# A norm factor spread over 128 partitions by a store and a load in place of a product with ones

## The chip, the cores and the metric

The kernel runs on one core of one Trainium2 chip. The metric is the device time of one execution in microseconds; lower is better. Three executions of the kernel before took 2622.88, 2625.9 and 2628.31 us; the median, 2625.9, stands for it.

## The reference

One layer over 4096 latent tokens of width 1024, with 256 context tokens ahead of it. Every token is normed by its root mean square, scaled and shifted, and goes through one wide projection, from which two branches take their parts: a gated MLP that mixes positions in chunks of 128, and a gated linear attention in both directions. The branches are merged by gates and go through an output projection. What matters here is the first line:

```python
def rmsnorm(x, g):
    xf = x.astype(jnp.float32)
    y = xf * lax.rsqrt(jnp.mean(xf * xf, axis=-1, keepdims=True) + EPS)
    return (y * g.astype(jnp.float32)).astype(x.dtype)
...
        h = rmsnorm(x, norm_g[layer]) * (1 + scale[:, None]) + shift[:, None]
        p = h @ wi
        hc = rmsnorm(xc, norm_g[layer]) * (1 + mod_c[D_MODEL:2 * D_MODEL]) + mod_c[:D_MODEL]
        pc = hc @ (wi[:, K0:ZB0] if last else wi)
```

Everything is in float32.

## The kernel before

The tokens are worked in 32 tiles of 128. **Stage 1** (to about 780 us) makes the normed input of each tile and from it the parts of the projection that the attention and the chunk mixing need; it also runs both. **Stage 2** makes the other parts of the projection and the output from halves that stage 1 writes to DRAM (opd). The change is in stage 1 alone.

In stage 1 each tile's input is on the chip twice: x (tokens on partitions, one buffer) and hf (channels on partitions, 8 blocks of 128 channels by 128 tokens, three buffers). The norm factor of a token is made from x, where a token's channels lie in one partition: a Square on ACT with a sum (L136) gives ms, one number per partition, and two POOL instructions (L88, L89) turn it into the reciprocal root. The products need it on hf, where tokens lie along the free axis, so all 128 factors have to be in every partition. `scales` puts them on a diagonal (dg, DVE, L139), and `spread` multiplies ones by that diagonal on PE (L144), which gives rb in PSUM: each partition holds all 128 factors. `modulate` then multiplies hf by rb on DVE (L149, all 8 blocks at once) and scales and shifts block by block on ACT (L151, 8 instructions). ms and dg have two buffers each, so a tile's Square (which writes ms) can't run before the diagonal of two tiles earlier has been made, and that one not before the rb of two tiles earlier has been multiplied.

`parts` (L165) copies hf into a rounded part hh (ACT, L167) and a rest hl (DVE, L168) for the products, and forms sums of halves that go to opd. PE's products l, v and a of a tile (L378 to L380, three instructions per block of channels) read hh and hl; k and q (L388 to L390) are made for two tiles at once. So the loop goes over **pairs of tiles**. For each pair: l of the even tile gives the low-rank gate inputs (stk, plr, lrT), those of both tiles give pg (PE, L424), then e (Exp and Ln on ACT), a scan, decays (em, kd, qdp, kdec), the masked scores (psc on PE, at on DVE), the attention's output po (PE, L608) with its copy oi, and the state: pk (PE), its copy sk (ACT, L615), and S (DVE, L619), from which the next sk is made. pr (PE, L547) and sv are the chunk mixing. Names in the rows: mk, mq, ml, mv, ma are the products k, q, l, v, a in PSUM; x, hf, ms, dg, rb carry their tile's number.

Each engine runs its instructions in the order in which they were laid down when the kernel was built. That order is made by the framework's scheduler from the program, the dependencies and the number of buffers, not written by hand; only some attention steps are tied to the last product ahead of them (`behind`). SP issues loads and most stores, ACT issues the stores of pkd and svd; each of these queues is in order too, so an instruction that waits holds up what stands behind it.

The 256 context tokens (`scales_T`, `norm_c`) use `spread` as well, twice, at the very start. From the outer program, the lines that start and drive this:

```python
            looked = {0: look(0)}
...
            if i:
                prepare(i + 1)
            pr0 = project(i, 0, lrT, "lva")
...
            kept["k", u] = heads("k", f"_{u}", lambda: behind(i - 2))
            stage(i - 1)
            kept["q", u] = heads("q", f"_{u}", lambda: behind(i - 2))
            behind(i - 1)
            prepare(i + 2)
            pr1 = project(i + 1, 1, lrT, "lva")
```

Of the kernel before, what the change touches and what calls it, by code (L numbers as in the profile page):

```python
# [8 lines left out]
F32 = mybir.dt.float32  # L9
F32R = mybir.dt.float32r  # L10
U32 = mybir.dt.uint32
AF = mybir.ActivationFunctionType
ALU = mybir.AluOpType

P = 128
# [3 lines left out]
NT = SEQ // P  # L19
# [18 lines left out]
def block_kernel(ctx: ExitStack, tc, t, out):  # L38
    nc = tc.nc
    V, S, G, T, Q = nc.vector, nc.scalar, nc.gpsimd, nc.tensor, nc.sync  # L40

    cp = ctx.enter_context(tc.tile_pool(name="cp", bufs=1))
    dr = ctx.enter_context(tc.tile_pool(name="dr", bufs=1, space=bass.MemoryType.DRAM))
# [9 lines left out]
    gated = dr.tile([KT, P], F32, name="gated")  # L53
    csd = dr.tile([2 * KT, P], F32, name="csd")
    xhd = dr.tile([SEQ, 256], F32, name="xhd")

    banks = {}

    def psum(tag, shape, name):
        pool, n = banks[tag]  # L60
        return pool.tile(shape, F32, tag=tag, name=name, bufs=n)
# [7 lines left out]
    def const(name, shape, dt=F32):  # L69
        c = cp.tile(shape, dt, name="c_" + name)  # L70
        Q.dma_start(c, t[name])
        return c
# [13 lines left out]
    def rstd_of(dst, n):  # L86

        G.tensor_scalar(dst, dst, EPS, None, ALU.add)  # L88
        G.tensor_tensor(dst, dst, mhalf[:, :n], ALU.pow)  # L89
# [6 lines left out]
    with ExitStack() as c1:  # L96
# [7 lines left out]
        ph = c1.enter_context(tc.tile_pool(name="ph", bufs=2))  # L104
# [20 lines left out]
        def load_x(src, srcT, name):  # L125

            x = ph.tile([P, D], F32, tag="x", name="x" + name, bufs=1)
            Q.dma_start(x, src)
            hf = ph.tile([P, KT, P], F32, tag="hf", name="hf" + name, bufs=3)
            Q.dma_start(hf, srcT)  # L130
            return x, hf

        def scales(x, name):

            ms = ph.tile([P, 1], F32, tag="ms", name="ms" + name)
            S.activation(x, x, AF.Square, scale=1.0 / 32.0, accum_out=ms)  # L136
            rstd_of(ms, 1)
            dg = ph.tile([P, P], F32, tag="dg", name="dg" + name)
            V.tensor_scalar(dg, ident, ms, None, ALU.mult)  # L139
            return dg  # L140

        def spread(dg, name):
            rb = psum("t", [P, P], "rb" + name)
            T.matmul(rb, lhsT=ones, rhs=dg, start=True, stop=True)  # L144
            return rb

        def modulate(hf, rb, who):

            V.tensor_tensor(hf, hf, rb.unsqueeze(1).to_broadcast([P, KT, P]), ALU.mult)  # L149
            for k in range(KT):  # L150
                S.activation(hf[:, k, :], hf[:, k, :], AF.Identity, bias=AB[:, 0, k, who:who + 1],  # L151
                             scale=AB[:, 1, k, who:who + 1])

        def look(i):
            x, hf = load_x(t["x"][i * P:(i + 1) * P, :], t["xT"][i], f"_{i}")
            return hf, scales(x, f"_{i}")

        def ready(i):
            if i + 1 < NT:
                looked[i + 1] = look(i + 1)  # L160
            hf, dg = looked.pop(i)
            modulate(hf, spread(dg, f"_{i}"), 0)
            return hf

        def parts(i, hf):  # L165
# [17 lines left out]
        def prepare(i):  # L183
            parts(i, ready(i))


        with ExitStack() as c0:
# [91 lines left out]
            for g in range(4):  # L279
# [24 lines left out]
                if g == 0:  # L304
                    ident = const("ident", [P, P])
# [22 lines left out]
            load_w1("v", 256, 512)  # L328
            load_w1("l", 0, 272)
            looked = {0: look(0)}  # L330
            Q.dma_start(msk, t["msk"])
            Q.dma_start(dmask, t["dmask"])
# [136 lines left out]
        for c0 in (0, 256):  # L469
            for j in range(2):  # L470
                pvv = product(j, "v", c0, c0 + 256, f"mvc{j}{c0}")
                S.copy(vs[j][:, c0:c0 + 256], pvv)
        hf0 = ready(0)
        for j in range(2):
            pl = product(j, "l", 0, 272, f"mlc{j}")
# [188 lines left out]
        i = NT - 2  # L664
# [276 lines left out]
    for b in reversed(range(NSUP)):  # L941
# [16 lines left out]
        for c in range(KT):  # L958
# [5 lines left out]
            i = b * ST + ST - 1 - c  # L964
# [117 lines left out]
    for n, (b, half) in enumerate(steps):  # L1082
# [9 lines left out]
        for c in range(KT):  # L1092
# [15 lines left out]
            if half:  # L1108
                f = mo[:, c]
# [6 lines left out]
            f = pf.tile([P, BTOK], F32, tag="f", name=f"fm{nm}_{c}")  # L1116
# [224 lines left out]
```

## Time and profile before

| What | Before |
|---|---|
| Median of 3 executions | 2625.9 us (2622.88 to 2628.31) |
| The profiled execution | 2625.88 us |
| Its span in the profile | 2624.1 us |
| PE's granted clock, mean | 0.993 |
| POOL, all of its work in the span | 542.5 us in 514 instructions |
| HBM, mean over the span | 184 GB/s |

The span is what the profiler saw between the first and the last instruction; 1.78 us of the execution lie around it. PE is the matmul engine and PEld its weight loads, DVE, ACT and POOL the vector, scalar and general engines, SP the one that issues DMAs; ACTq and SPq in a row are those engines' instruction queues (a DMA issue stands there). A row of a timeline has start, length, engine, line, operation, output and inputs, shape and count, and in brackets how long the engine had been idle and what released it; a row of groups has count, busy time, mean length in ns, and idle time ahead of it. Lengths of matmuls overlap, as one starts before the last has drained; so on PE the distance between two starts is what one costs. A product of 128 x 128 by 128 x 272 starts about 0.127 us behind the last.

### The profile page before, as it was taken

How to read it: one execution, taken by the hardware profiler on the slowest of the kernel's cores; microseconds unless marked ns; L12 is line 12 of the kernel's file. 1: busy time of each engine (PE TensorE's matmuls, PEld its weight loads, DVE VectorE, ACT ScalarE, POOL GpSimd, SP SyncE). 2: the span in 40 equal slices, each digit the busy share in tenths (PEclk: the TensorE clock that was granted, in tenths of full speed). 3: DMA queues.
4: the chain of work that ended last, by engine and by line, in shares of the span. 5: the costliest groups of instructions: out<-in, count | busy, mean ns of one | idle time of the engine just before them, and what ended most of it. 6: DMA issues, size and time to landing. Idle time of an engine off the chain costs nothing.

```text
span 2624.1 us, 37671 instructions
## 1 busy us (share of the span) xinstructions
PE 2571.3 (98%) x13688; PEld 2202.0 (84%) x13688; DVE 1758.1 (67%) x2980; ACT 1213.1 (46%) x2478; POOL 542.5 (21%) x514
## 2 busy tenths in 40 slices
PE   8999999999988999999999999999999999999998
PEld 4899999999987778888888888888878888878887
DVE  6677777777787656775578557855678666565555
ACT  5666665656564444454445443544441011144443
POOL 2101010000002333233223333333310000032222
PEclk9999999999999999999999999999999999999999
DMA  8443434343349554554446444644359968676654
GB/s 287 152 137 128 144 125 153 125 152 120 119 128 253 197 181 155 194 208 154 135 160 229 153 150 150 229 149 164 121 192 338 340 223 271 232 258 222 224 201 145
DMA packets 248956, 485.37 MB, mean 185 GB/s; under 512 B 20551, under 2 KB 127327, under 8 KB 235074
## 3 DMA queue, kind: packets, MB, share of 16 engines
q1 hardware_dynamic: 189922, 416.88, 47.5%
q10 hardware_dynamic: 58848, 66.08, 7.6%
q8 instruction: 108, 1.77, 0.3%
q14 instruction: 78, 0.64, 0.1%
HBM read 303.56 MB, written 179.32 MB: 184 GB/s over the span
## 4 chain that ended last, share of the span: by engine, by line
PE 62%; DMA 4%; DVE 2%; issue 1%; ACT 1%; POOL 1%; SPq 0%; POOLq 0%; DVEq 0%; ACTq 0%
PE Xg L753 12%; PE Xa L753 6%; PE Wg L753 6%; PE poX L1188 6%; PE py L1037 4%; PE py L1035 4%; PE py L1036 4%; PE poW L1188 3%; PE Xz L753 3%; PE Wa L753 3%; PE Yg L753 3%; PE Wz L753 2%; PE Ya L753 1%; PE poY L1188 1%; DMA op<-opd 1%; PE po L849 1%
## 5 line engine op out<-in xcount | busy, mean ns | idle before, releaser
L1188 PE MATMUL poX<-wo,mop 128*128 128x512 f32 x768 | 176.2, 390 | 2.0 <-DVE mop L1179 2.0
L1188 PEld LDWEIGHTS poX<-wo,mop 128*128 128x128 f32 x768 | 144.0, 188 | 32.7 <-DVE mop L1179 2.8
L1194 POOL TENSOR_TENSOR so<-so,xo 128x512 f32<-128x512 f32 x48 | 71.3, 1500 | 418.4 <-ACT so L1193 366.6
L727 POOL TENSOR_TENSOR rg<-rg 128x512 f32<-128x512 f32 x32 | 46.3, 1447 | 399.3 <-DMA rg<-in_wq 352.0
L1106 DVE TENSOR_TENSOR sg<-sg,py 128x512 f32<-128x512 f32 x128 | 86.6, 683 | 62.0 <-PE py L1037 60.5
L1179 DVE TENSOR_TENSOR mop<-mr,mop 128x1024 fp32r<-128x1024 f32 x56 | 73.2, 1307 | 70.3 <-ACT mop L1178 69.9
L151 ACT ACTIVATE hf<-hf,AB 128x128 f32<-128x128 f32 x256 | 102.4, 481 | 29.3 <-DVE hf L149 29.3
L1025 ACT CAST ah<-al 128x512 fp32r<-128x512 f32 x32 | 17.6, 618 | 210.2 <-DMA al<-abd 144.8
L378 PE MATMUL mv<-w_vh,hh 128*128 128x512 f32 x256 | 101.7, 397 | 0.6 <-ACT va L524 0.6
L1037 PE MATMUL py<-bh,wbl 128*128 128x512 f32 x256 | 99.7, 390 | 0.9 <-DVE wbl L1016 0.9
L1035 PE MATMUL py<-bh,wbh 128*128 128x512 f32 x256 | 100.0, 390 | 0.7 <-ACT wbh L1015 0.6
L380 PE MATMUL mv<-w_vh,hl 128*128 128x512 f32 x256 | 100.1, 391 | 0.0
L379 PE MATMUL mv<-w_vl,hh 128*128 128x512 f32 x256 | 100.1, 391 | 0.0
L1036 PE MATMUL py<-bl,wbh 128*128 128x512 f32 x256 | 99.7, 389 | 0.0
L1035 PE MATMUL py<-ah,wbh 128*128 128x512 f32 x256 | 99.7, 389 | 0.0
L1037 PE MATMUL py<-ah,wbl 128*128 128x512 f32 x256 | 99.6, 389 | 0.0
L1036 PE MATMUL py<-al,wbh 128*128 128x512 f32 x256 | 99.6, 389 | 0.0
L753 PE MATMUL Xg<-op,w1g 128*128 128x512 f32 x384 | 97.9, 404 | 0.5 <-DVE w1g L749 0.5
L753 PE MATMUL Xg<-op,w6g 128*128 128x512 f32 x384 | 93.3, 391 | 5.1 <-ACT s1g L758 4.9
L753 PE MATMUL Wg<-op,w5g 128*128 128x512 f32 x384 | 94.0, 391 | 3.4 <-ACT w5g L748 2.1
L753 PE MATMUL Yg<-op,w2g 128*128 128x512 f32 x384 | 93.8, 390 | 0.0
L753 PE MATMUL Xg<-op,w7g 128*128 128x512 f32 x384 | 92.8, 390 | 0.0
(418 smaller groups left out, 7732.3 us busy)
## 6 DMA issues: line engine op xcount, KB each, us to landing
rg<-in_wq SPq DMA_DIRECT2D x32, 1024.0 KB, 5.5
gd<-fg SPq DMA_DIRECT2D x128, 256.0 KB, 2.4
sg<-gd SPq DMA_DIRECT2D x64, 512.0 KB, 4.8
op<-opd SPq DMA_DIRECT2D x28, 1024.0 KB, 5.9
mr<-md SPq DMA_DIRECT2D x56, 512.0 KB, 3.6
opd<-hf SPq DMA_DIRECT2D x80, 256.0 KB, 2.7
x<-in_x SPq DMA_DIRECT2D x32, 512.0 KB, 3.5
hf<-in_xT SPq DMA_DIRECT2D x32, 512.0 KB, 3.7
```

The source lines that it names most:

```text
L151: S.activation(hf[:, k, :], hf[:, k, :], AF.Identity, bias=AB[:, 0, k, who:who + 1], scale=AB[:, 1, k, who:who + 1])
L378: T.matmul(pp, lhsT=hh[:, j, k, :], rhs=wh[:, k, c0:c1], start=k == 0, stop=False)
L379: T.matmul(pp, lhsT=hh[:, j, k, :], rhs=wl[:, k, c0:c1], start=False, stop=False)
L380: last[0] = T.matmul(pp, lhsT=hl[:, j, k, :], rhs=wh[:, k, c0:c1], start=False, stop=k == KT - 1)
L753: T.matmul(pp, lhsT=w[:, wi, k, :], rhs=o[:, oi, :, k, :], start=first and k + i == 0, stop=k == 3 and i == 2, skip_group_check=not first)
L1035: T.matmul(pp, lhsT=wh[:, k, c0:c0 + P], rhs=ah[:, k, :], start=k == 0, stop=False)
L1036: T.matmul(pp, lhsT=wh[:, k, c0:c0 + P], rhs=al[:, k, :], start=False, stop=False)
L1037: last[0] = T.matmul(pp, lhsT=wl[:, k, c0:c0 + P], rhs=ah[:, k, :], start=False, stop=k == 3)
L1106: V.tensor_tensor(sg[:, z], sg[:, z], py[z], ALU.mult)
L1179: V.tensor_tensor(o[:, 1], raw, o[:, 0].bitcast(F32), ALU.subtract)
L1188: T.matmul(pp, lhsT=o[:, oi, k, :], rhs=w[k // 2][:, wi, k % 2, :], start=begin and k + i == 0, stop=k == 3 and i == 2, skip_group_check=n ...
L1194: G.tensor_tensor(s, s, xs[r][:, half, halves[z]], ALU.add)
```

## The change

For the 32 token tiles, the diagonal and the product with ones go. ms is stored to DRAM by ACT, 128 numbers of 4 bytes into a tile `rsd[i]` of its own, and loaded back by SP with a broadcast, so that each of the 128 partitions receives all 128 numbers. rb now lies in SBUF and takes the two buffers that dg had. The context tokens keep `spread`. `scales` is dissolved into `look`.

```diff
+    rsd = [dr.tile([P], F32, name=f"rsd{i}") for i in range(NT)]
...
-        def scales(x, name):
-
-            ms = ph.tile([P, 1], F32, tag="ms", name="ms" + name)
-            S.activation(x, x, AF.Square, scale=1.0 / 32.0, accum_out=ms)
-            rstd_of(ms, 1)
-            dg = ph.tile([P, P], F32, tag="dg", name="dg" + name)
-            V.tensor_scalar(dg, ident, ms, None, ALU.mult)
-            return dg
-
...
         def look(i):
+
             x, hf = load_x(t["x"][i * P:(i + 1) * P, :], t["xT"][i], f"_{i}")
-            return hf, scales(x, f"_{i}")
+            ms = ph.tile([P, 1], F32, tag="ms", name=f"ms_{i}")
+            S.activation(x, x, AF.Square, scale=1.0 / 32.0, accum_out=ms)
+            rstd_of(ms, 1)
+            S.dma_start(rsd[i].rearrange("(p a) -> p a", a=1), ms)
+            rb = ph.tile([P, P], F32, tag="dg", name=f"rb_{i}")
+            Q.dma_start(rb, rsd[i].partition_broadcast(P))
+            return hf, rb
 
         def ready(i):
             if i + 1 < NT:
                 looked[i + 1] = look(i + 1)
-            hf, dg = looked.pop(i)
-            modulate(hf, spread(dg, f"_{i}"), 0)
+            hf, rb = looked.pop(i)
+            modulate(hf, rb, 0)
             return hf
```

On all engines the order of stage 1 is laid down anew. Three places follow, with the numbers of tiles and chunks in the names.

**In a pair, DVE, from a chunk's decays to its scores.** Before: kdec of chunk 9, the state S of chunk 8, and the scores at of chunk 9, with the product of hf[12] inside; the product of hf[13] comes ten rows on, among the rows of sp.

```order
L587 TENSOR_TENSOR kdec_9_3593<-kd_9_3585,decs_119 128x512
L420 MEMSET sp_5_3808 128x8
L619 SCALAR_TENSOR_TENSOR S_8_3637<-S_7_3235,decs_119,pk_8_3628 64x128 x4
L614 TENSOR_TENSOR sk_9_3762<-S_8_3637,decs_119 64x512
L598 TENSOR_TENSOR at_9_3671<-psc0_9_3672,dmask_167 128x256
L601 COPY_PREDICATED at_9_3671<-pmask_168,psc0_9_3672 64x2x64 x2
L598 TENSOR_TENSOR at_9_3671<-psc1_9_3680,dmask_167 128x256
L149 TENSOR_TENSOR hf_12_3360<-hf_12_3360,rb_12_3705 128x1024
L601 COPY_PREDICATED at_9_3671<-pmask_168,psc1_9_3680 64x2x64 x2
L139 TENSOR_SCALAR dg_14_3897<-c_ident_213,ms_14_3893 128x128
```

After, at the same place:

```order
L586 TENSOR_TENSOR kdec_9_3614<-kd_9_3606,decs_151 128x512
L419 MEMSET sp_5_3828 128x8
L141 TENSOR_TENSOR hf_13_3718<-hf_13_3718,rb_13_3725 128x1024
L141 TENSOR_TENSOR hf_14_3911<-hf_14_3911,rb_14_3918 128x1024
L618 SCALAR_TENSOR_TENSOR S_8_3658<-S_7_3257,decs_151,pk_8_3649 64x128 x4
L613 TENSOR_TENSOR sk_9_3782<-S_8_3658,decs_151 64x512
L597 TENSOR_TENSOR at_9_3692<-psc0_9_3693,dmask_199 128x256
L600 COPY_PREDICATED at_9_3692<-pmask_200,psc0_9_3693 64x2x64 x2
L597 TENSOR_TENSOR at_9_3692<-psc1_9_3701,dmask_199 128x256
```

The products of both tiles of a pair, hf[13] and hf[14], now stand side by side between kdec and S, outside at and sp, and the rb that they read comes by DMA.

**In a pair, ACT, from k to lrT.** Before: the copies of k and q and of chunk 10, kdT, all 8 blocks of hf[14], and at the end of the stretch a Square, v and lrT.

```order
L402 ACTIVATE k_6_4097<-mk_6_4024 64x2x256 x4
L585 DMA pkd11_75<-qdp1_175 64x4x128
L610 COPY oi_10_4156<-po_10_4151 128x512
L611 DMA pkd10_74<-oi_10_4156 128x512
L615 COPY sk_10_4164<-pk_10_4159 64x512
L616 DMA pkd10_74<-sk_10_4164 128x512
L402 ACTIVATE q_6_4197<-mq_6_4126 64x2x256 x4
L446 COPY kdT_11_4224<-pkt_11_4219 128x512
L151 ACTIVATE hf_14_3891<-hf_14_3891,AB_171 128x128 x8
...
L136 ACTIVATE x_18_4951,ms_18_4955<-x_18_4951 128x1024
L520 COPY v_13_4327<-mv_13_4302 128x512
L415 CAST lrT6_3888<-plr_13_4329 98x128
```

After, at the same place one pair earlier:

```order
L401 ACTIVATE k_5_3587<-mk_5_3514 64x2x256 x4
L143 ACTIVATE hf_13_3718<-hf_13_3718,AB_203 128x128 x4
L609 COPY oi_8_3646<-po_8_3641 128x512
L143 ACTIVATE hf_13_3718<-hf_13_3718,AB_203 128x128
L610 DMA pkd8_72<-oi_8_3646 128x512
L614 COPY sk_8_3654<-pk_8_3649 64x512
...
L615 DMA pkd9_73<-sk_9_3782 128x512
L143 ACTIVATE hf_14_3911<-hf_14_3911,AB_203 128x128 x2
L150 ACTIVATE x_30_8141,ms_30_8145<-x_30_8141 128x1024
L152 DMA rsd30_145<-ms_30_8145 128x1
L519 COPY v_11_3816<-mv_11_3791 128x512
L414 CAST lrT5_3379<-plr_11_3818 98x128
```

The blocks of both tiles stand here, 16 in all, scattered between the copies of k, oi, sk and q (the other tile's 8 stood behind the second Ln of e before), and the store of rsd[30] stands directly behind its Square and ahead of v and lrT. In this kernel four pairs have five Squares each (x[10] to x[29]) and one more has two (x[30] and x[31], when tile 14 is worked on); later pairs have none, where before each pair had two. SP's loads of rb stand a pair ahead of the products that read them, behind a load of x and ahead of stores to opd.

**At the end of stage 1, PE.** Before: the last rows of ml[30], then plr and pr, and ml[31] behind them.

```order
L378 MATMUL ml_30_8690<-w_lh_138,hh_178 128x272
L379 MATMUL ml_30_8690<-w_ll_139,hh_178 128x272
L380 MATMUL ml_30_8690<-w_lh_138,hl_179 128x272
L414 MATMUL plr_30_8720<-c_ident_213,stk0_172 98x128
L547 MATMUL pr_29_8723<-wsT_169,xh_29_8640 128x128 x2
L378 MATMUL ml_31_8754<-w_lh_138,hh_178 128x272
L379 MATMUL ml_31_8754<-w_ll_139,hh_178 128x272
L388 MATMUL mk_15_8831<-hh_178,w_qkh_143 128x256
L388 MATMUL mq_15_8931<-hh_178,w_qkh_143 128x256
```

After, ml[31] and 15 rows of mk stand ahead, then the scores of chunk 28 and the same plr and pr:

```order
L388 MATMUL mk_15_8831<-hl_211,w_qkh_175 128x256
L389 MATMUL mk_15_8831<-hh_210,w_qkl_176 128x256
L594 MATMUL psc0_28_8731<-qdp0_206,kd_28_8659 128x128
L595 MATMUL psc0_28_8731<-qdp0_206,kdx0_208 128x64
L594 MATMUL psc0_28_8731<-qdp0_206,kd_28_8659 128x128
L595 MATMUL psc0_28_8731<-qdp0_206,kdx0_208 128x64
L594 MATMUL psc1_28_8739<-qdp0_206,kd_28_8659 128x128
L595 MATMUL psc1_28_8739<-qdp0_206,kdx0_208 128x64
L594 MATMUL psc1_28_8739<-qdp0_206,kd_28_8659 128x128
L595 MATMUL psc1_28_8739<-qdp0_206,kdx0_208 128x64
L413 MATMUL plr_30_8720<-c_ident_245,stk0_204 98x128
L546 MATMUL pr_29_8723<-wsT_201,xh_29_8642 128x128 x2
```

PE's l product of tile 31 (24 instructions) has moved from behind plr[30] to ahead of it; on ACT the 8 blocks of hf[31] have moved ahead with it.

**At the start, SP.** After, with the first load of rb:

```order
L334 DMA lng_202<-in_lng 128x4
L338 DMA w2r_480<-in_w2s 98x512
L340 DMA sel_482<-in_sel 98x1
L154 DMA rb_0_473<-rsd0_115 128x128
L271 DMA r_qk0_499<-in_w1qk 128x8x256
L355 DMA csd_113<-csr_496 16x128
L264 DMA r_a00_505<-in_w1a 128x1088
L264 DMA r_a04_509<-in_w1a 128x1088
```

The load of rb[0] is new; before, r_qk followed sel at once.

## The prediction

> **What bounds the kernel now.** I read the engine shares first, then the windows, to find what limits the stretch in which the 32 token tiles are normed (about 60 to 780 us), then that stretch's timelines.
>
> ```profile
> PE 2571.3 (98%) x13688; PEld 2202.0 (84%) x13688; DVE 1758.1 (67%) x2980; ACT 1213.1 (46%) x2478; POOL 542.5 (21%) x514
> 60.00:150.00 90.00, 87.16 (x624) 81.51 (x623) 59.86 (x119) 60.06 (x133) 15.38 (x22) 0.98 0.47 155
> 150.00:240.00 90.00, 90.00 (x665) 85.50 (x664) 66.30 (x151) 56.84 (x127) 8.24 (x16) 1.00 0.41 135
> ...
> 600.00:690.00 90.00, 90.00 (x664) 85.54 (x663) 66.39 (x152) 55.77 (x124) 8.24 (x16) 1.00 0.41 132
> 690.00:780.00 90.00, 85.49 (x640) 82.26 (x639) 72.47 (x164) 52.63 (x114) 3.30 (x6) 0.96 0.35 110
> ```
>
> The window columns are the stretch, its length, and the busy time of PE, PEld, DVE, ACT and POOL, then PE's granted clock, the DMA share and GB/s. From 150 to 690 us PE is busy 90.00 us of 90.00 at clock 1.00. Whatever leaves PE there shortens the time one for one, as long as the other engines keep up. DVE (66) and ACT (57) have room on average; whether they have it at the right moment is the whole question. Only at the end, from 690, does PE idle 4.5 us.
>
> **The matmuls that go.** These rows are the group of removed matmuls, then PE's own timeline around one of them: start, length, engine, line.
>
> ```profile
> L144 PE MATMUL rb<-dg,ones x64: 272/275/422, 59.5 to 739.9; 128*128 128x128 f32 x64
> 159.05 0.29 PE L380 MATMUL ma<-w_ah,hl 128*128 128x272 f32 x1
> 159.17 0.38 PE L144 MATMUL rb<-dg,ones 128*128 128x128 f32 x2
> 159.31 0.37 PE L378 MATMUL ml<-w_lh,hh 128*128 128x272 f32 x1
> 159.52 0.29 PE L379 MATMUL ml<-w_ll,hh 128*128 128x272 f32 x1
> 203.84 0.38 PE L144 MATMUL rb<-dg,ones 128*128 128x128 f32 x2
> ```
>
> The 64 instructions are 32 matmuls of two passes. Lengths overlap, so the cost is read from starts. The rb starts 0.12 after the ma ahead of it, as an ml would have; the next ml starts 0.14 after rb, and the one behind that 0.21 later, where its neighbours come at 0.13. That is 0.14 + 0.08 = 0.22 us each, 32 x 0.22 = **7.07 us off PE**. From 159.17 to 203.84 is one pair of tiles: 44.67 us, holding two rbs. A pair that stays bound by PE would take 44.23.
>
> The 32 diagonals on DVE go too (first row below, 0.28 us each); DVE is not what PE waits for in these windows, so I count nothing. The product hf x rb now reads SBUF and not PSUM. The nearest rows of the same size are the product as it is and hl, which is all in SBUF:
>
> ```profile
> L139 DVE TENSOR_SCALAR dg<-c_ident,ms x32: 254/280/290, 52.9 to 699.2; 128x128 f32<-128x128 f32 x32
> L149 DVE TENSOR_TENSOR hf<-hf,rb 128x1024 f32<-128x1024 f32 x32 | 38.9, 1217 | 12.8 <-PE rb L144 12.8
> L168 DVE TENSOR_TENSOR hl<-hf,hh 128x1024 fp32r<-128x1024 f32 x32 | 38.8, 1214 | 13.6 <-ACT hh L167 13.6
> ```
>
> 1217 against 1214 ns: no change.
>
> **The round trip that comes.** Store and load do not exist in the profile. The nearest rows are a small store to DRAM and the load that spreads it again over the partitions (size, us from issue to landing):
>
> ```profile
> csd<-csr SPq DMA_DIRECT2D x1, 8.0 KB, 2.8
> crow<-csd SPq DMA_DIRECT2D x4, 128.0 KB, 3.2
> 332.77 0.22 POOL L88 TENSOR_SCALAR ms<-ms 128x1 f32<-128x1 f32 x1 [20.80 <-ACT x L136]
> 333.07 0.57 POOL L89 TENSOR_TENSOR ms<-ms,mhalf 128x1 f32<-128x1 f32 x1
> ```
>
> From the Square's end (332.68, quoted below) POOL takes until 333.64, 0.96 us; then an issue, 2.8, another issue, 3.2: about 7.5 us from Square to spread factors. In the order of after, the store frees ms early, so x loads and Squares run far ahead: x[30] is squared while tile 14 is modulated, and rb[13] and rb[14] are issued on SP ahead of the work of their pair. The trip has tens of microseconds, so it costs no time in steady state. The Trainium skill, in "DMA: Bandwidth & Descriptors", section "Rules for kernel authors", says the opposite about such transfers taken alone: below 64 KB one pays mostly overhead. The csd row's 2.8 us for 8 KB agrees with that; what it would do here if it were on the path is the third rival.
>
> What does cost is the issue. ACT issues the store, and its queue is in order: where the store stands directly behind its Square, ACT stands for POOL's 0.96 us plus an issue (0.34 in ACT's rows below), 1.3 to 1.5 us. Behind it are v and lrT, and PE's pg needs lrT. SP's rb loads wait for the product of the pair before; behind them are opd stores and x loads, which nobody needs soon.
>
> **The ACT stretch that decides.** One pair of before, on ACT from the end of k to lrT, with PE's pg that follows:
>
> ```profile
> 317.58 1.80 ACT L402 ACTIVATE k<-mk 64x512 f32<-64x512 f32 x3
> 319.40 0.59 ACT L610 COPY oi<-po 128x512 f32<-128x512 f32 x1
> 320.02 0.34 ACTq L611 DMA_DIRECT2D pkd<-oi  x1
> 320.46 0.58 ACT L615 COPY sk<-pk 64x512 f32<-64x512 f32 x1 [0.47 <-ACT oi L610]
> ...
> 321.45 2.40 ACT L402 ACTIVATE q<-mq 64x512 f32<-64x512 f32 x4 [0.41 <-PE mq L390]
> 323.88 0.59 ACT L446 COPY kdT<-pkt 128x512 f32<-128x512 f32 x1
> 325.50 3.19 ACT L151 ACTIVATE hf<-hf,AB 128x128 f32<-128x128 f32 x8 [1.03 <-DVE hf L149]
> ...
> 328.74 1.05 ACT L167 CAST hh<-hf 128x1024 fp32r<-128x1024 f32 x1
> 329.69 0.35 ACT L516 COPY va<-ml 128x240 f32<-128x240 f32 x1
> ...
> 331.53 1.06 ACT L136 ACTIVATE x<-x 128x1024 f32<-128x1024 f32 x1 [0.40 <-ACT sk L615]
> 332.49 0.19 ACT L136 ACTIVATION_READ_ACCUMULATOR x<-x 128x1 f32 x1
> 333.81 0.59 ACT L520 COPY v<-mv 128x512 f32<-128x512 f32 x1 [1.13 <-PE mv L380]
> 334.29 0.27 ACT L415 CAST lrT<-plr 98x128 fp32r<-98x128 f32 x1
> 334.61 0.38 PE L424 MATMUL pg<-lrT,W2b 98*128 98x256 f32 x1
> ```
>
> In before this stretch holds eight hf pieces and ACT rests in it (0.41, 1.03, 1.13 us). In after both tiles' hf pieces stand here, sixteen, and a Square with its store. Summed back to back: hf 2 x 3.19 = 6.4; oi and sk twice, 2.3; q 2.4; kdT 0.6; hh 1.0; stk and va 0.5; Square 1.1; the stand for POOL and the issue 1.4; v and lrT 0.8: **16.5 us**, or 16.1 where neighbours overlap. From k's end at 319.0 to 319.4 it ends at 335.1 to 335.9. PE, having lost up to 0.44 us of work, would like pg at 334.2 to 334.6. So lrT is late by **0.8 to 1.5 us; I take 1.2**, as the sum lies nearer the middle than either end. How often? The order holds five Squares per pair in four pairs and two in a fifth, then none are left, since x[31] is done near tile 15. So five pairs: +6 us (4 to 7.5).
>
> In the other nine or so pairs the Square and its stand (2.5 us) are absent; ACT is then a microsecond or more early, and I count nothing. The price if that cover is gone is the second rival.
>
> **DVE's place.** In after, the two products stand together between kdec and S.
>
> ```profile
> 321.07 1.11 DVE L619 SCALAR_TENSOR_TENSOR S<-S,decs,pk 64x128 f32<-64x128 f32 x4 [3.31 <-ACT sk L615]
> ...
> 324.25 1.21 DVE L149 TENSOR_TENSOR hf<-hf,rb 128x1024 f32<-128x1024 f32 x1
> 325.38 0.61 DVE L601 COPY_PREDICATED at<-pmask,psc 64x128 f32<-64x128 uint32 x2
> 326.33 0.50 PE L608 MATMUL po<-v,at 128*128 128x128 f32 x3
> ```
>
> DVE idled 3.31 us there for sk; two products (2.43) fit. Four to six hf pieces of 0.4 now stand ahead of sk on ACT, so S starts about 2.2 us later, but the product no longer stands inside the at group (1.21 less). at ended at 325.99, 0.34 before po. Now: 325.99 + 2.2 - 1.2 = 327.0 by this crude count, and about 325.6 to 325.9 when k's earlier end and the pieces' overlap are followed instruction by instruction. PE's wish is 325.9. It fits, barely: zero, with up to 0.9 per pair at risk.
>
> **Both ends of the stage.** At the end of it, the only long wait of PE:
>
> ```profile
> 747.67 0.45 PE L414 MATMUL plr<-c_ident,stk 128*98 128x128 f32 x1 [4.42 <-DVE stk L410]
> 741.52 3.19 ACT L151 ACTIVATE hf<-hf,AB 128x128 f32<-128x128 f32 x8 [0.89 <-DVE hf L149]
> ```
>
> PE ran out of ml at 743 and stood until 747.67, since hf[31] had only been modulated from 741.5 to 744.7 and stk came behind. In after hf[31] is modulated about a third of a pair earlier, and the 24 ml of tile 31 and 15 mk stand ahead of that plr. I take **-3.5** of the 4.4; 0 if something else is late there. At the start, SP's load of rb[0] waits for its store's landing and stands ahead of this load:
>
> ```profile
> 50.36 0.55 SPq L272 DMA_DIRECT2D r_qk<-in_w1qk  x1
> 84.84 0.28 PE L388 MATMUL mk<-hh,w_qkh 128*128 128x256 f32 x1
> ```
>
> It slips by 5 to 6 us, while the first product with those weights is 34 us away; also the first products wait for 7.5 us where the matmul needed 1.5. I take **+0.7** (0 to 1.5).
>
> **The sum**, against the profiled execution's 2625.88 us (span 2624.1 and 1.78 around it; it equals the median, 2625.9): 2625.88 - 7.07 - 3.5 + 0.7 + 6.0 = **2622.0**. With the ends of the terms: 2618.4 to 2627.8.
>
> **Rivals.**
> 1. ACT keeps up: the sixteen pieces overlap so well that lrT is never late. For: ACT's mean share is 57 of 90. Against: the sum of 16.5 us. It would give 2625.88 - 7.07 - 4.4 + 0.7 = 2615, or 2616 with the end stall as I took it.
> 2. Slower: the chain ACT sk, DVE S, at, PE po becomes what PE waits for in every pair. For: the crude count above put at a microsecond late, and slack is 0.34 us. Against: the finer one. With a cost c in each of some 15 pairs the sum is 2625.88 - 9.9 + 15c; it breaks even at c = 0.66 and is slower by 0.2% from c = 1.0. At 1.3 it gives 2635.5.
> 3. The round trip lands on the path. At the start alone that adds 6 us to my sum: 2628. In each tile it would be 32 x (2.8 + 3.2) = 192 us, about 2815; the order speaks against that, with a look-ahead of more than ten tiles, and so do the hidden pkd stores of before. The Trainium skill's overhead rule named above points the same way as this rival, and its price is worked out here from the two rows.
>
> **Chances.** My case 0.46, of which 0.10 lies below 2620.6; rival 1 0.25; rival 2 0.16, nearly all slower; rival 3 0.13, nearly all the small form within 0.2%. About 0.2%, 5.25 us, is what a measurement of this kernel can tell from no change. Faster: 0.10 + 0.25 = 0.35. Slower: 0.14 + 0.02 = 0.16. Same: 0.49. The range for 8 in 10 goes from rival 1's lower end, 2614, to 2633, between rival 2's break-even and its 2635.5; what is left out is the dearer half of rivals 2 and 3 and little below.
>
> **What would show it.** Right: no rb matmul; pairs without Squares take 44.2 us from one pair's first ml to the next; five pairs, up to the one with x[31], take about 45.4, with PE waiting for lrT from ACT; no 4.4 us wait before plr at the end; the waits of DVE hf on the load at zero past the first pair. Wrong: PE waits for at, or for sk through S, in later pairs (rival 2); PE full throughout (rival 1); hf waiting on the rb load, or a wait on w_qk near 85 us (rival 3). The forecast fails most easily at the 16.5 us sum: half a microsecond in it moves the total by 2.5.

## The result and the profile after

The changed kernel takes **2760.9 us** (median of four executions, 2749.6 to 2765.1) against 2627.1 for the kernel before (four executions, one more than in the table ahead); the ratio is **1.049** (95% interval 1.048 to 1.051). The profiled execution is the shortest of the four: 2749.62 us, span 2747.8, 123.7 more than the span before. The forecast was 2622, with a range up to 2633.

First the shares of the engines and some windows of the kernel after, with the columns of the prediction's first fence.

```profile
PE 2606.3 (95%) x13624; PEld 2231.8 (81%) x13624; DVE 1747.3 (64%) x2948; ACT 1223.3 (45%) x2478; POOL 551.4 (20%) x514
...
150.00:240.00 90.00, 69.57 (x473) 66.28 (x472) 48.85 (x108) 41.06 (x89) 12.06 (x22) 0.87 0.69 135
240.00:330.00 90.00, 77.41 (x520) 72.28 (x519) 51.96 (x117) 55.74 (x121) 10.93 (x22) 0.94 0.67 128
330.00:420.00 90.00, 75.66 (x519) 72.32 (x519) 50.67 (x115) 48.52 (x102) 10.45 (x20) 0.91 0.83 141
420.00:510.00 90.00, 85.50 (x598) 80.83 (x598) 61.54 (x136) 50.89 (x113) 7.39 (x12) 0.96 0.37 115
...
600.00:690.00 90.00, 85.65 (x614) 81.00 (x613) 60.86 (x137) 52.32 (x114) 5.80 (x8) 0.98 0.34 109
```

Two things are to be seen. To 420 us, as long as there are Squares and stores (the last store is issued at 433), PE works 70 to 77 us of 90, and the DMA share is 0.67 to 0.83 at the bytes per second at which it was 0.41 before. Behind that no store is left, the DMA share is normal, and still PE misses some 4.4 us of 90, at a clock of 0.96 to 0.98.

A table made from PE's timelines shows where the 123.7 us arise. k[n] is the start of the first k product of pair n.

| Stretch | Before, us | After, us | More |
|---|---|---|---|
| to k[0] | 84.8 | 102.5 | 17.7 |
| k[0] to k[1] | 41.9 | 53.3 | 11.4 |
| k[1] to k[6], five pairs with Squares | 223.3 | 291.3 | 68.0 |
| k[6] to k[14], eight pairs without | 357.4 | 383.5 | 26.1 |
| k[14] to the first product Xg of stage 2 | 118.6 | 115.0 | -3.6 |
| from there to the end | 1798.0 | 1802.2 | 4.2 |

In the changed kernel, as in all that take its order, twelve products of stage 2 (Wg, from 931.0 us) stand ahead of the first Xg; in before they come behind it.

**The store.** The view of its line, with the issues and its landing:

```profile
L152 ACTq DMA_DIRECT2D rsd<-ms x32: 326/326/359, 52.1 to 433.3; - x32
...
DMA to landing us min/median/max: 7.8/9.0/11.3
```

The list of DMA issues, with the median landing last in each row; the first row is that of before, the others are those of the changed kernel:

```profile
x<-in_x SPq DMA_DIRECT2D x32, 512.0 KB, 3.5
...
x<-in_x SPq DMA_DIRECT2D x32, 512.0 KB, 8.8
...
rb<-rsd SPq DMA_DIRECT2D x32, 64.0 KB, 3.2
```

And waits from the lists of ACT and DVE (total, times, longest):

```profile
ACT x L150 <- DMA x<-in_x: 48.3, 13, 12.3
...
DVE hf L141 <- DMA hf<-in_xT: 44.1, 9, 6.6
...
DVE hf L141 <- DMA rb<-rsd: 22.4, 4, 10.5
```

512 bytes take 9.0 us to land, three times as long as the 8 KB of csd. The load of rb takes the expected 3.2. But the x loads, which nobody changed, rose from 3.5 to 8.8 us, and ACT stood 48.3 us for them. DVE stood 44.1 us for loads of hf: from 100 to 450 us SP held these back 37.7 us until the opd stores out of the same buffers had landed, against 4.5 in before. Neither wait is in the lists of before. Not every transfer suffered: the pkd stores of oi, which ACT issues, kept their 2.0. What PE then waits for, from 100 to 450 us (in before its list for this stretch is empty):

```profile
PE plr L413 <- DVE stk L409: 27.9, 7, 8.7
PE psc L594 <- ACT oi L609: 12.6, 4, 4.4
```

In ACT's timeline one sees how a late x travels:

```profile
205.63 1.06 ACT L150 ACTIVATE x<-x 128x1024 f32<-128x1024 f32 x1 [8.27 <-DMA x<-in_x]
...
219.66 1.06 ACT L150 ACTIVATE x<-x 128x1024 f32<-128x1024 f32 x1 [0.33 <-DMA x<-in_x]
220.63 0.18 ACT L150 ACTIVATION_READ_ACCUMULATOR x<-x 128x1 f32 x1
...
225.30 0.34 ACTq L152 DMA_DIRECT2D rsd<-ms  x1
...
226.29 0.63 ACT L570 ACTIVATE em<-sp 128x512 f32<-128x512 f32 x1 [4.17 <-DVE xh L533]
```

A Square stands for its x for 8.27 us. Of the later Square, at 219.66, the store is issued only 4.5 us behind the Square's end, with svd's store and em queued behind it on ACT. In the trace this issue waits until 225.24 for the semaphore on which the store issued at 213.35 reports its landing, so the slow store also holds ACT itself.

**The pairs without stores.** DVE's, ACT's and PE's timelines in one of them:

```profile
583.25 0.17 DVE L567 COPY sm<-pf 128x4 f32<-128x4 f32 x1
583.33 0.69 DVE L175 TENSOR_TENSOR hf<-hf 128x512 f32<-128x512 f32 x1
583.93 0.68 DVE L573 TENSOR_TENSOR kd<-k,em 128x512 f32<-128x512 f32 x1
584.53 1.40 DVE L583 TENSOR_TENSOR qdp<-q,sp 64x512 f32<-64x512 f32 x2
585.96 0.69 DVE L586 TENSOR_TENSOR kdec<-kd,decs 128x512 f32<-128x512 f32 x1
586.57 0.68 DVE L176 TENSOR_TENSOR hf<-hf,hf 128x512 f32<-128x512 f32 x1
587.17 0.18 DVE L409 TENSOR_TENSOR stk<-ml,stk 128x32 fp32r<-128x32 f32 x1
...
578.97 0.19 ACT L408 CAST stk<-ml 128x32 fp32r<-128x32 f32 x1
...
585.04 0.29 PE L378 MATMUL ma<-w_al,hh 128*128 128x272 f32 x1
587.50 0.42 PE L413 MATMUL plr<-c_ident,stk 128*98 128x128 f32 x1 [2.17 <-DVE stk L409]
```

ACT's half of stk is done at 579.2. DVE's half, 0.18 us long, stands behind sm, a sum of the odd tile (L175), kd, qdp, kdec and a second sum (L176), and comes at 587.2. PE's plr waits 2.17 us for it. In before DVE's stk stood directly behind sm, ahead of kd and of all four sums:

```profile
300.78 0.17 DVE L568 COPY sm<-pf 128x4 f32<-128x4 f32 x1
300.86 0.18 DVE L410 TENSOR_TENSOR stk<-ml,stk 128x32 fp32r<-128x32 f32 x1
...
303.25 0.69 DVE L574 TENSOR_TENSOR kd<-k,em 128x512 f32<-128x512 f32 x1
```

### The profile page after: what moved, and what is told of

Read it like the earlier page. It is cut to its first block, busy times and chain, and to the rows that moved or that the text cites. A ratio compares the mean times of both kernels' runs of the same rounds, so it can differ in the third digit from the quotient of the medians.

```text
span 2747.8 us, 37631 instructions
## 1 busy us (share of the span) xinstructions
PE 2606.3 (95%) x13624; PEld 2231.8 (81%) x13624; DVE 1747.3 (64%) x2948; ACT 1223.3 (45%) x2478; POOL 551.4 (20%) x514
## 4 chain that ended last, share of the span: by engine, by line
PE 58%; DMA 5%; DVE 2%; ACT 1%; issue 1%; SPq 0%; POOL 0%; DVEq 0%; POOLq 0%; ACTq 0%
PE Xg L752 11%; PE Xa L752 6%; PE Wg L752 5%; PE poX L1187 5%; PE py L1036 4%; PE py L1035 4%; PE py L1034 4%; PE poW L1187 3%; PE Xz L752 3%; PE Yg L752 3%; PE Wa L752 3%; PE Wz L752 2%; PE Ya L752 1%; DMA gw<-in_wgate 1%; PE poY L1187 1%; DMA op<-opd 1%
## 5 line engine op out<-in xcount | busy, mean ns | idle before, releaser
L143 ACT ACTIVATE hf<-hf,AB 128x128 f32<-128x128 f32 x256 | 111.8, 488 | 28.0 <-DVE hf L141 22.5
L530 POOL TENSOR_SCALAR rs<-mvar 128x1 f32<-128x1 f32 x32 | 22.4, 700 | 462.8 <-DVE mvar L528 459.2
```

## The experiments

Two theories. **S**: the store of 4-byte pieces costs, by its landing and by what it does to other transfers. **O**: the new order costs, in the pairs without stores too. The next table holds the medians of the runs that cross the two; the others are told below. Runs 2, 3, 4 and 6 leave the token factors out of the result, and serve for their times alone.

| | order of the changed kernel | sums placed later |
|---|---|---|
| 4-byte stores, five per pair (the changed kernel) | 2760.9 | 2728.2 |
| 4-byte stores, two per pair | 2698.2 | 2670.3 |
| no store and no load | 2667.4 | 2629.7 |

The kernel before took 2627.1 to 2629.6 beside them.

**1. The store alone, in the order of before.**

```diff
             rstd_of(ms, 1)
+            S.dma_start(rsd[int(name[1:])].rearrange("(p a) -> p a", a=1), ms)
             dg = ph.tile([P, P], F32, tag="dg", name="dg" + name)
```

> The kernel before with one thing added: ACT stores ms of every token tile to DRAM (128 words of 4 bytes), and nobody reads it. The order of everything else is that of before. Theory S (the store itself is what costs: in the changed kernel it took 9.0 us to land and the x loads rose from 3.5 to 8.8 us): the store again lands in 8 to 10 us, x loads take over 5 us, and the time rises by 20 us or more. Theory O (the new order of stage 1 costs, not the store): the store may land late, but PE stays full from 150 to 690 us, pairs stay at 44.7 us, and the time is 2626 within 5.

2650.9 us, ratio 1.009 (1.007 to 1.011). The store lands in 8.1 us (for the x loads this trace has no landing), and PE's busy time from 240 to 330 us falls from 90.00 to 89.63. The list of landings for opd and xhd, which were 2.7 and 1.7 before:

```profile
opd<-hf SPq DMA_DIRECT2D x80, 256.0 KB, 7.1
...
xhd<-xh SPq DMA_DIRECT2D x32, 128.0 KB, 4.5
```

A store that nobody reads makes its neighbours land in some 2.6 times their time. In mid-stage that costs only 0.25 us per pair; 18 us arise up to k[1]. Theory S named the size of the total, but what it costs lies at the start; in mid-stage, in the order of before, it costs nearly nothing, as O has it.

**2 and 3. The order alone: ones in place of the factors, and then loads without stores.**

```diff
-            S.dma_start(rsd[i].rearrange("(p a) -> p a", a=1), ms)
-            rb = ph.tile([P, P], F32, tag="dg", name=f"rb_{i}")
-            Q.dma_start(rb, rsd[i].partition_broadcast(P))
-            return hf, rb
+            return hf, ones
```

> The changed kernel without store, load and spreading at all: hf is multiplied by a constant tile of ones (the token factors are left out of the result; Squares and the two POOL instructions stay). Its order has Squares far ahead and DVE's stk behind kdec, as in the changed kernel. Theory S: 2612 to 2620, pairs 44.2 us. Theory O: the pairs without Squares keep 48.1 us, and the whole loss of some 134 us stays but for the start: over 2730. Theory S and O together: every pair about 48 us from the second on, 14 x 3.4 = 48 more than before, less some 6 at the end: 2665 to 2680.

> The changed kernel without its stores: SP still loads rb for every tile with a broadcast, but from one constant row (the token factors are left out of the result). Theory S: about 2615 to 2625. Theory O: over 2730, as the order is nearly that of the changed kernel. S and O together: 2665 to 2685, within 10 us of the run without loads, x loads back at 3 to 5 us.

2667.4 (1.015, interval 1.012 to 1.019) and 2661.4 us (1.013, 1.011 to 1.015), the second a little under its range. With no transfer added, the later pairs take 48.1 us, as in the changed kernel: PE's plr waits for stk 25.6 us in 12 pairs. So the order alone costs some 33 to 39 us, and the loads nothing. What is left of the 134 us needs the stores.

**4. The same store in pieces of 64 bytes.**

```diff
-            S.dma_start(rsd[i].rearrange("(p a) -> p a", a=1), ms)
+            S.dma_start(rsd[i], msw[i % 2])
```

> The changed kernel with the store widened from 4 to 64 bytes per partition (16 words, only the first is a factor); the load reads the first 512 bytes of it, so the factors in the result are replaced. Number of pieces and order are those of the changed kernel. If the cost of the store lies in pieces of 4 bytes (several written within one 64-byte line): it lands in 2 to 4 us and the time is that of the run without stores, 2665 to 2685. If it lies in the number of small pieces, whatever their size: it lands in about 9 us and the time stays at 2745 to 2765. Theory O alone: 2745 to 2765 with either landing time.

2671.1 us (1.017, 1.015 to 1.019). Sixteen times the bytes land in 3.2 us and the x loads in 4.0; the 90 us are gone. It isn't the number of pieces.

**5 and 9. What makes a small store slow.** Two ladders, each the kernel before with one extra store per tile in eight forms, four stores of a form, one execution each.

> The kernel before with one extra store per token tile, issued by ACT behind the diagonal dg and taken from its first columns; nobody reads it. Eight forms take turns, four tiles each: a4 = 128 pieces of 4 bytes side by side in DRAM (as in the changed kernel), p64 and p512 = 4 bytes each, 64 or 512 bytes apart, a16, a32, a64 = 128 pieces of 16, 32, 64 bytes side by side, q128 = 4 pieces of 128 bytes, s4 = 4 bytes into each partition of an SBUF tile. Measured: us from issue to landing. Theory L (several small writes to one 64-byte line of DRAM wait for each other): a4 8 to 10 us, a16 4 to 6, a32 3 to 5, and p64, p512, a64, q128, s4 all 2 to 3.5. Theory N (any piece under 64 bytes to DRAM is slow, wherever it lies): a4, p64, p512, a16, a32 all 7 us or more, s4 2 to 3. Theory C (128 tiny pieces are slow anywhere): s4 too.

> The kernel before with one extra store per token tile, taken from dg as in the first ladder, again eight forms in turn. all = 128 words side by side (as in the changed kernel), na, nb, nc = the same with 16, 32, 64 words, pa, pb, pc = 128 words 8, 16, 32 bytes apart, w = 128 pieces of 8 bytes side by side. The first ladder gave 8.2 us for 128 words side by side and 2 for every other form. Theory R (pieces that fall into one 512-byte stretch of DRAM wait for each other, some 60 ns each): all 8, nc 4 to 5, nb 2 to 3, na 2, pa and w (64 pieces per 512 bytes) 4 to 5, pb 2 to 3, pc 2. Theory G (only a gapless run of 4-byte words is slow): pa, pb, pc and w all 2, nc 4 to 5, nb 2 to 3.

The lists of DMA issues: first the first ladder (rsp is p64 and p512 together; rsa are a4, a16 and a64; rss is SBUF; a32 and q128 have no landing in it), then the second.

```profile
rsp<-dg ACTq DMA_DIRECT2D x8, 0.5 KB, 2.0
...
rsa<-dg ACTq DMA_DIRECT2D x4, 0.5 KB, 8.2
rss<-dg ACTq DMA_DIRECT2D x4, 0.5 KB, 1.7
rsa<-dg ACTq DMA_DIRECT2D x4, 2.0 KB, 1.9
...
rsa<-dg ACTq DMA_DIRECT2D x4, 8.0 KB, 1.9
```

```profile
rsall<-dg ACTq DMA_DIRECT2D x4, 0.5 KB, 8.8
rsna<-dg ACTq DMA_DIRECT2D x4, 0.1 KB, 1.3
rsnb<-dg ACTq DMA_DIRECT2D x4, 0.1 KB, 5.4
rsnc<-dg ACTq DMA_DIRECT2D x4, 0.2 KB, 7.9
rspa<-dg ACTq DMA_DIRECT2D x4, 0.5 KB, 4.9
rspb<-dg ACTq DMA_DIRECT2D x4, 0.5 KB, 1.4
rspc<-dg ACTq DMA_DIRECT2D x4, 0.5 KB, 2.0
rsw<-dg ACTq DMA_DIRECT2D x4, 1.0 KB, 4.7
```

Four bytes are not slow by themselves: into SBUF, or 16 bytes and more apart, they land in 1.4 to 2.0 us. 128 of them side by side take 8 to 9, at 8 bytes' distance or as 8-byte pieces 4.7 to 4.9. So it is **how closely the pieces lie in DRAM** that decides, and how many there are, as 16 words side by side land in 1.3. Theory N and theory C fall, G too. L and R named the right direction with wrong numbers: L had 16-byte pieces side by side slow, and they weren't; R had the time in proportion to the number of words, and it isn't (16, 32, 64, 128 words: 1.3, 5.4, 7.9, 8.8). Which unit makes them wait isn't shown.

The Trainium skill, in "DMA: Bandwidth & Descriptors", section "Specifications", says that transfers below 512 bytes are done by reading, changing and writing back. The slow forms fit such a rule, but the fast ones (16 bytes each, or 64 bytes apart) are below 512 bytes as well, so by these runs the rule alone doesn't tell which store is slow.

**6. The cause of the later pairs.** The four sums (L175 to L178, taken out of `parts`) are written behind the first step of the even tile, which makes l and stk; everything else is as in experiment 2. The row behind it is a window of its profile.

```diff
             next(pr0)
+            if i:
+                sums()
             next(pr0)
```

> The run with a constant tile of ones in place of the token factors (no store, no load, no spreading), with one change of order: the four sums of the odd tile that go to opd are written in the program behind the even tile's l product, so that DVE's stk of the even tile stands ahead of them. Theory O (the sums, kd, qdp and kdec ahead of stk on DVE are what makes PE wait 2.2 us per pair at plr, and its clock halves behind that): PE's wait at plr goes, pairs 44.2 to 44.4 us, clock 1.00, total 2610 to 2622. Rival A (ACT's stretch from k to lrT is what is too long): pairs stay above 46 and the total above 2645, with the wait moved to pg.

```profile
420.00:510.00 90.00, 90.00 (x668) 85.60 (x667) 65.56 (x147) 54.25 (x119) 4.88 (x8) 1.00 0.35 112
```

PE is full, its clock 1.00, and each of the eight later pairs takes 44.23 us, the figure that the prediction gave for a pair bound by PE. Theory O holds, rival A falls. But the total, 2629.7, is that of before (0.9998, 0.9987 to 1.0010) and above the expected range: stage 1 ended only 2.3 us earlier in the profiled execution, since k[1] came 4.2 us later than before and the next five pairs took 0.1 to 1.2 us more than 44.23; stage 2 took 6 us more. Stage 2's order on PE is the same as in the changed kernel, and as in before but for its first 26 us, and its length differs by several us between kernels (its first block took 288 to 294 us in the profiles of this study); what sets it wasn't looked into.

**7, 8 and 11. Bursts and their sum with the order.** In 7, ms becomes a 129th column of rb's buffer, so that a Square waits for the product of two tiles earlier and stores come two per pair; 8 is the changed kernel with the sums later; 11 is both.

```diff
-            ms = ph.tile([P, 1], F32, tag="ms", name=f"ms_{i}")
+            rbm = ph.tile([P, P + 1], F32, tag="dg", name=f"rb_{i}")
+            rb, ms = rbm[:, 0:P], rbm[:, P:P + 1]
```

> The changed kernel, with ms as a 129th column of rb's buffer, so that a tile's Square waits until the product of two tiles earlier is done: Squares and 4-byte stores come two per pair, as in before, and not five. Theory B (stores in bursts of five per pair delay the x loads, and with them ACT): start 15 to 18 us late, then about 48 us per pair as in the run with ones, total 2680 to 2700. Rival (each 4-byte store costs its share in this order wherever it falls): the 60 us that stores cost in pairs 1 to 6 are spread over all pairs, which take 51 to 53 us, total 2740 to 2770.

> The changed kernel whole, with only the order of the four sums changed as in the run with ones and sums later. Theory O and S add up: the later pairs take 44.3 us (8 x 3.8 = 30 less), those with five stores lose a part of their stall too: 2705 to 2730. If the two have one cause (the order only hurts because stores delay something), the later pairs stay at 48 and the total over 2745.

> The changed kernel with Squares two per pair and the four sums behind the even tile's l product; stores stay at 4 bytes a piece. Theory O (the order of DVE's stk is the cost of every later pair): 14 pairs lose 3.6 us each, 2640 to 2655, pairs 44.2 to 44.5 us. Rival (4-byte stores now show in every pair, since PE's stall no longer covers them): pairs 45 to 47, 2660 to 2690.

7: 2698.2 us (1.026), as theory B has it: k[0] at 104.6 and k[1] at 158.4, 2 to 3 us later than in the changed kernel, then 47.8 us per pair. The burst was worth 63 us. 8: 2728.2 (1.038, 1.036 to 1.039), as S and O together have it; the later pairs take 44.23. Those with stores take 50 to 71; they were expected to lose a part of their stall and didn't: k[1] to k[6] take 300 us, 9 more than in the changed kernel. 11: 2670.3 (1.016), and here the rival was right: from k[2] on the pairs take 44.4 to 49.1, most of them 45, and PE's list of waits from 160 to 740 us has

```profile
PE pg L426 <- ACT lrT L417: 10.7, 11, 3.3
```

Where PE no longer stands for stk, it stands for lrT on ACT, the stretch of the prediction, now with a store per pair in it. The two costs aren't quite additive: one covers a part of the other.

**10. The start.** Tiles 0 to 3 spread by the product with ones, stores from tile 4 on, two per pair, order of the changed kernel.

> The changed kernel with Squares two per pair (ms in rb's buffer), and the first four tiles spread by the product with ones as before; tiles 4 to 31 by store and load. The run with two per pair and no such exception took 2698, some 30 more than the run with ones, all of it ahead of the third pair. Theory P (at the start the round trip is on the path: hf waits for rb, and the load of rb[0] holds r_qk): 2665 to 2678. Rival (the early stores hold up the loads of the start, as in the run that adds stores to before, wherever rb comes from): 2685 or more.

2690.7 us (1.023), in the rival's range: theory P falls as it stood. But the rival's delay of the start doesn't show: k[0] came at 85.9, nearly as before. The next two pairs took 52.9 and 54.6; hf waited there for rb 11.0 us in two waits, where in run 7 it had waited 23.1 us in four. The delay moves to the first tiles that use the store, wherever these are.

**12 to 15. Versions with all three mended.** The factors are turned on DVE, so that 128 words lie as four rows of 32, and SP stores four pieces of 128 bytes; two Squares per pair, sums later. Tiles below FIRST are spread by the product with ones.

```diff
+            G.tensor_tensor(x[:, 0:1], ms, mhalf[:, :1], ALU.pow)
+            V.transpose(x[:, 32:64], x[:, 0:32])
+            Q.dma_start(rsd[i].rearrange("(q a) -> q a", a=32), x[0:P:32, 32:64])
             Q.dma_start(rb, rsd[i].partition_broadcast(P))
```

> A version that mends all three suspected costs: Squares two per pair, the sums behind the even tile's l product, the first four tiles spread by the product with ones, and for tiles 4 to 31 the factors turned on DVE in blocks of 32 x 32, so that SP stores 4 pieces of 128 bytes and loads them back with a broadcast. If the three causes are all there is: pairs 44.2 us, no late start, stage 1 some 8 to 10 us shorter than before: 2614 to 2622. Rival (stage 2 gives part of it back, as it did by 6 us in the run with ones and sums later): 2622 to 2630.

> The version with 4 pieces of 128 bytes, Squares two per pair and the sums later, with no tile spread by the product with ones. If the cost at the start is the slow 4-byte store and not the round trip as such: start 3 to 6 us late (as with 64-byte pieces), no disturbed pair later, pairs 44.2: 2617 to 2627. Rival (a round trip of 7 us is on the path at the start for several tiles, whatever the piece): start 15 us or more late, 2630 or more.

> The same with tile 0 alone spread by the product with ones, so that no store's landing stands ahead of the r_qk load on SP. Reading 1 (the delay of r_qk is the cost at the start): the first k product starts within 1 us of before, pairs 45 then 44.2, 2614 to 2623. Reading 2 (the switch from product to round trip costs some 5 us at whichever tile it comes, as it did at tile 4): 2622 to 2630.

> The same with tiles 0 to 7 spread by the product with ones. Reading 1: the start and the first pairs as in before, then 44.2 us per pair for 11 pairs and 6 us less at the end, 2615 to 2623. Reading 2 (the switch costs 5 us wherever it comes): one disturbed pair around tile 8, 2622 to 2630.

| FIRST | median, us | ratio (interval) | k[0] | k[4] | a later pair |
|---|---|---|---|---|---|
| 4 | 2628.4 | 0.9999 (0.9987 to 1.0011) | 84.6 | 269.3 | 44.20 |
| 0 | 2640.2 | 1.0038 (1.0025 to 1.0052) | 88.6 | 278.6 | 44.20 |
| 1 | 2636.2 | 1.0024 (1.0015 to 1.0033) | 83.8 | 276.3 | 44.20 |
| 8 | 2640.8 | 1.0035 (1.0022 to 1.0047) | 86.8 | 274.6 | 44.20 |

Before had k[4] at 260.8 and pairs of 44.67; the k columns are of one profiled execution each (of FIRST 0, the slowest of its five). With all three mended the loss of 134 us is gone but for 1 to 11 us. The start is at most 4 us late, also with FIRST 0, where runs 7 and 11 with 4-byte stores were 20 late; so at k[0] it was the 4-byte store and not the round trip (run 4, with 64-byte pieces issued by ACT, had k[0] at 88.9). But each version is 8 to 18 us late by k[4], mostly from the two or three pairs near its first round trip, and the rest of stage 1 at best wins that back. So the three causes aren't all there is: runs 12 and 13 ended in their rivals' ranges, though not by the rivals' mechanisms (with FIRST 4 stage 2 was as long as before, with FIRST 0 the start wasn't 15 us late). Reading 1 holds for the start alone; reading 2 holds in kind, at a higher price than the 5 us it named.

The trace of FIRST 0 shows the wait in the disturbed pairs. ACT's order has two Squares there, and the second starts at 166.03 after 4.40 us of idle, 5 us after SP issued the load of its x (160.80). That load stood on SP behind the store of the factors out of the same buffer x and the load of rb; v and lrT stand behind the Square, and PE waits 3.62 us for lrT. It comes again one pair on (4.27 us of idle, 3.19 of PE). ACT stands for x with FIRST 1 and 8 too (10.4 and 9.0 us in all), hardly with FIRST 4 (0.7). No run tests this. No version tried beats the kernel before.

## Why the prediction was wrong

- **32 products, 7.07 us off PE: right.** A pair bound by PE takes 44.20 to 44.23 us in runs 6, 8 and 12 to 15; the prediction said 44.23.
- **The round trip, "costs no time in steady state": wrong, and the largest error.** The term was sized by csd, 8 KB in 2.8 us, as the nearest row. It was the nearest small store, but csd has 16 pieces of 512 bytes and the new store 128 of 4, side by side. The store took 9.0 us, and what no term held is that it slowed other transfers (x 3.5 to 8.8 us). With store and load out, nearly the same order takes 2667, with them 2761: some 94 us.
- **That look-ahead hides it: wrong in sign.** The run of Squares ahead was read as cover. It put five stores into each early pair, where Squares, x loads and the opd stores stand behind slow landings; with two per pair the same kernel takes 63 us less. Rival 3 had the place at the start and "6 us"; k[1] came 29 us late.
- **DVE, "it fits, barely: zero": wrong, by a row that was not looked at.** The prediction followed kdec, S, at and po, which held in the later pairs. The earlier products let the odd tile's sums, kd, qdp and kdec be placed ahead of the even tile's stk. That cost 3.9 us in each later pair against 44.23, 2.2 of them waiting and the rest in a slower clock (below). Run 6 shows it by one move in the program. Rival 2 had the sign and some of the size, with another mechanism: sk, S, at is not what PE waits for.
- **ACT's stretch, 1.2 us in five pairs: not shown.** In run 6, with three to five Squares in each of these pairs but no store for ACT to stand for, k[1] to k[6] take 224.5 us, 3.3 more than five times 44.23, and lrT isn't in PE's list of waits there (stk is, with 1.9 us). So the sixteen pieces and the Squares alone don't make lrT late. In run 11, with a store in every pair, lrT is what PE waits for, 10.7 us in eleven waits. In the sum, the lateness was given as 0.8 to 1.5, while its own two ends (335.1 to 335.9 against 334.2 to 334.6) give 0.5 to 1.7.
- **The end, -3.5: the wait right, the number partly luck.** The 4.4 us wait is gone and k[14] to Xg is 3.6 us shorter. But in before 6.83 us at a clock of 0.50 followed that wait (746.74 to 753.57), which the term didn't hold, and in after twelve Wg products stand ahead of Xg, which it didn't hold either.
- **The start, +0.7: wrong.** r_qk was issued 8.9 us later, not 5 to 6, but ACT waited only 0.47 us for it. What was late was hf, which stood three times for rb, 20.3 us in all, in DVE's timeline:

```profile
65.52 1.22 DVE L141 TENSOR_TENSOR hf<-hf,rb 128x1024 f32<-128x1024 f32 x1 [10.54 <-DMA rb<-rsd]
...
91.22 1.22 DVE L141 TENSOR_TENSOR hf<-hf,rb 128x1024 f32<-128x1024 f32 x1 [5.27 <-DMA rb<-rsd]
...
99.88 1.23 DVE L141 TENSOR_TENSOR hf<-hf,rb 128x1024 f32<-128x1024 f32 x1 [4.48 <-DMA rb<-rsd]
```

The first k product needs the rests hl of two tiles, and the second of them (101.63) stands on DVE behind the third wait. So rival 3 had the wait right and its price, 6 us, too low.

## What to carry to other kernels

Size a new transfer by the row with the same pieces, not the same bytes: here 128 words side by side in DRAM took 9 us and slowed loads and stores beside them, and four pieces of 128 bytes, made by one turn on DVE, took that away. When a change lets work run ahead, ask which single buffer it queues at, and what it is now placed in front of: the whole row order of the short instructions that the bound engine waits for (here a 0.18 us stk) has to be read, not only the moved ones. Where one engine is at 90 of 90 us, taking a quarter of a percent off it is easily less than what the new order costs.

## What the runs showed of the hardware

A short stall can cost more than its length, since PE's clock falls behind it. Of the eight later pairs of the changed kernel seven took 48.0 to 48.3 us, and one took 46.6, though its stall is as long as that at 587.50 above:

```profile
635.63 0.29 PE L413 MATMUL plr<-c_ident,stk 128*98 128x128 f32 x1 [2.17 <-DVE stk L409]
```

Four windows of 3.41 us, two around each of the two stalls:

```profile
584.10:587.51 3.41, 1.24 (x10) 1.01 (x10) 3.35 (x7) 1.61 (x5) 0.00 (x0) 1.00 0.49 130
587.51:590.92 3.41, 3.41 (x16) 3.41 (x17) 3.40 (x7) 0.50 (x2) 0.00 (x0) 0.50 0.66 218
631.88:635.30 3.42, 1.58 (x11) 1.28 (x9) 3.36 (x6) 1.84 (x4) 0.00 (x0) 1.00 0.38 109
635.30:638.71 3.41, 3.08 (x26) 3.11 (x27) 3.41 (x8) 0.62 (x3) 0.00 (x0) 1.00 0.66 202
```

The windows are not chosen freely. In the trace's clock records every fall from 444 to 830 us lasts 3.41 us at 0.50, and the falls begin at whole multiples of 3.41 us from each other (from 587.51 to 683.08 are 28). So the clock is set here for one stretch of 3.41 us after another, on a fixed grid. Where a whole stall lies in one stretch, PE is busy 1.23 to 1.37 us of it and the next stretch runs at 0.50, with 16 products at 587.51. The stall ahead of 635.63 lies across a border of the grid: PE is busy 1.58 us of the stretch, the clock stays at 1.00, and 26 products are done in the next. In runs 2 and 4 the one late pair of 46.6 us has its stall across a border too (1.57 and 1.65 us busy). So the limit lies here between 1.37 and 1.57 us busy of 3.41, and a fall costs about 1.5 us.

The Trainium skill, "TensorE: Matmul & The Clock Gate", Part 1, says that activity is watched over free-running windows of about 3.4 us, and gives as its abstract rule that no PE idle gaps above some 3.4 us be left. The windows agree with this trace. The rule, taken as a limit, does not: here 2.04 to 2.18 us of idle within one window were enough.
